# Padding three pools of a three-block transformer kernel so that its tiles begin on multiples of 256 bytes

## The chip, the core and the metric

The kernel runs on one core of a Trainium2 chip, as one launch. The metric is the time of the launch in microseconds on the device. The engines are TensorE (PE in the rows; PEld is its loading of stationary operands), VectorE (DVE), ScalarE (ACT), GpSimd (POOL) and SyncE (SP, which issues most DMAs).

## What is computed

A hybrid mixer layer and two layers of a two-stream transformer, in float32, for 256 tokens of width 1024, plus a second stream of 256 context tokens. Cut to its products, with `rms` the RMS norm:

```
h = x + mixer(rms(x))              # dilated attention, state space scan, gates: w_in, w_attn, w_ssm, w_out
h = h + (silu(n @ w_gate) * (n @ w_up)) @ w_down          # n = rms(h), inner width 2816
x = rms(h)
for layer in (0, 1):
    x, c: half a swiglu                                    # both streams
    x, c: attention (layer 0: windowed and differential; layer 1: latent and neighbourhood)
    x (c in layer 0): half a swiglu
# each part is scaled, shifted and gated by vectors from silu(cond) @ w_mod
```

Nearly all of the arithmetic is products of a weight matrix with 256 tokens.

## The kernel before

**Products.** A weight matrix is cut into slabs: 128 output features with all of their 1024 inputs (or 768, or fewer), 4096 bytes on each of 128 partitions. A slab is loaded into `wraw` (line 102, SyncE), and `split_w` makes two float32r parts of it: `wh` by a cast on ScalarE (line 109) and `wl` by a subtraction on VectorE (line 110). Activations are held feature-major as two such parts too (`ahx` and `alx` for the stream x, `ahc` and `alc` for the context, `hh` and `hl` for the hidden layer of a swiglu, `yn`, `ao` and a few others). `mm3_k` multiplies them: for each block k of 128 inputs three products go to one PSUM tile, `wh·ah` (line 128), `wh·al` (line 129) and `wl·ah` (line 130). In each the 128x128 block of the weight is the stationary operand (512 bytes a partition) and 256 tokens of one block of the activations are the moving one (1024 bytes a partition). Each of the three loads its own stationary operand.

**Order.** `run` takes units (a slab and what is done with it) in order and prepares slabs two units ahead; `wraw`, `wh` and `wl` have five buffers each. With two streams each slab serves 48 products, with one 24. Attention, scan, norm and the vectors of the modulation (line 938, VectorE) are woven in between units. A scheduler sets the order on each engine; it doesn't look at addresses.

**Places.** Tiles are taken from pools, which lie in SBUF one behind the other: `cst` (constants: `ones`, `cols`, `ident`, `tri`, the `mcol` vectors), `raw`, `wsplit`, `tmp`, `small`, then the pools of the streams and of each stage, stacked. Where a tile starts follows from the sizes of all before it. The program's data begins at byte 16,512 of each partition, `cst` is 5,184 bytes long, so `raw` begins at 21,696, which is 84 times 256 and 192 over. In the code that the change touches, `Builder.__init__` (line 68) makes the first pools, `rstd_cols` (line 274) uses `small`, `block1` (line 408) makes `b1x` with `cw` and `half`, and `mix_cd` makes `dqg`.

The end of a branch unit is a place that the prediction uses: `ssm_unit` (line 819) multiplies the 16 blocks of the group norm in one go, 12 of them in the tiles `yn` and the last 4 in `ao_h` and `ao_l`.

Of the kernel before, what the change touches and what calls it, by code (L numbers as in the profile page):

```python
# [8 lines left out]
F32 = mybir.dt.float32  # L9
F32R = mybir.dt.float32r  # L10
AF = mybir.ActivationFunctionType
ALU = mybir.AluOpType
AX = mybir.AxisListType
PSUM = bass.MemoryType.PSUM
# [30 lines left out]
class Unit:  # L45
    """n weight slabs of src from index `at`, and what is done with them for each stream."""
# [5 lines left out]
def weave(units, steps, start=0, stop=0):  # L52
    """The steps spread evenly between the units, from the unit start on, up to stop units before the end."""
    n = len(units) - start - stop
    out, done = list(units[:start]), 0
    for i, u in enumerate(units[start:]):
        out.append(u)
        upto = min(len(steps), -(-len(steps) * (i + 1) // max(n, 1)))
        out += steps[done:upto]
        done = upto  # L60
    return out + list(steps[done:])


class Builder:
# [19 lines left out]

    def pool(self, ctx, name, bufs):
        return ctx.enter_context(self.tc.tile_pool(name=name, bufs=bufs))
# [12 lines left out]
    # ---------------------------------------------------------------- weights  # L99
# [17 lines left out]
    def mm3(self, out, w, acts, m=128, first=True, last=True):  # L117
        """out[m, t] += sum over k of w[k, m] * act[k, t], each factor as the sum of two float32r parts."""
        n = len(acts)
        for k in range(n):  # L120
            self.mm3_k(out, w, acts, k, m, first and k == 0, last and k == n - 1)
# [14 lines left out]
    def stream(self, s, src):  # L136
        """A stream of tokens, feature-major: the residual and what goes into the next product."""
        self.act_p[s] = self.pool(self.ctx, "act" + s, 1)
        self.X[s] = self.act_p[s].tile([128, KB, T], F32, name="x" + s)
        for b in range(KB):  # L140
            self.nc.sync.dma_start(self.X[s][:, b], src[:, b])
# [9 lines left out]
    def lin(self, src, i, acts, evac, m=128, streams=None):  # L151
        """A unit of work: the product of slab i of src with acts(stream), feature-major, to evac(stream, psum)."""
        return Unit(src, i, 1, None, streams, (acts, m, evac))

    def later(self, f, key=None):
        """f is issued behind the next unit of work: TensorE does not wait for what f needs."""
        self.deferred.append((key, f))

    def step(self):
        """What was put off so far."""  # L160
        todo, self.deferred = self.deferred, []
        for _, f in todo:
            f()

    def flush(self, keys=None):
        """What was put off, or only what belongs to the keys, is issued now."""
        while True:
            todo = [d for d in self.deferred if keys is None or d[0] in keys]
            if not todo:
                return  # L170
            self.deferred = [d for d in self.deferred if d not in todo]
            for _, f in todo:
                f()

    def run(self, items, streams, done=None, ko=0, ahead=2):
        """Units in order; the second stream follows the first at a distance, so that the end of one hides
        behind the other. The first ko units go k-outer in the last stream, while its activations are being made.
        Items that are no units are just called."""
# [76 lines left out]
    def background(self, n=1):  # L255
        """The next n pieces of the modulation vectors."""
        for _ in range(min(n, len(self.bg))):
            self.bg.pop(0)()
# [4 lines left out]
    # ------------------------------------------------------------------ norms  # L263
# [10 lines left out]
    def rstd_cols(self, p, n, scale, eps, newton=False):  # L274
        """1 / sqrt(p * scale + eps) of [128, n] sums of squares, a token to a partition."""
# [6 lines left out]
        if newton:  # L282
            # one step on 1 / sqrt(v): r * (1.5 - 0.5 * v * r * r)
# [7 lines left out]
    def sums(self, key):  # L291
        """The sums of squares with a token to a partition."""
# [6 lines left out]
    def on_all(self, r):  # L299
        """A column for each 128 tokens -> the same row on every partition, in PSUM."""  # L300
# [6 lines left out]
    def rstd_all(self, key, width, eps=1e-6):  # L307
        """1 / sqrt(mean of squares + eps) of each token, on every partition (in PSUM)."""
        return self.on_all(self.rstd_cols(self.sums(key), 2, 1.0 / width, eps))

    def norm(self, s, src, scale, shift, h, lo, r):
        """(src * scale) * r + shift of each block, as float32r parts."""
# [10 lines left out]
    def norm_stream(self, s, scale, shift, final=None):  # L323
        """The normed and modulated stream, for the next products; behind the next two units of work.
        final: the gain of a norm of the residual itself that comes first (the sums of its squares: s + "f")."""
# [37 lines left out]
    # -------------------------------------------------------------------- ffn  # L363
    def ffn(self, wg, wu, wds, streams, gate, hid_p, steps, done, after=None):
# [28 lines left out]
        # what a product down needs is ready some units before it  # L393
# [12 lines left out]
# ==================================================================== block 1  # L406
def block1(K, start_mod):
# [8 lines left out]
    # ---- the bias of each head of the dilated attention as a row over the distance, 32 times: read back with  # L416
    # a row pitch shorter by one, it is a Toeplitz tile
# [18 lines left out]
    cw = xpool.tile([128, 120], F32, name="cw")  # L436
# [13 lines left out]
    DIL = (1, 4, 16)  # L450
    o_t = y_t[1:]  # until the convolution needs the place
# [51 lines left out]
    def attend(g, b):  # L503
        """Two heads of a group."""
# [64 lines left out]
    # ---- the weights of the three groups: exp(m_g - max) / sum of den_g * exp(m_g - max)  # L569
    comb = {}  # L570

    def combine_rows():
        # in places that the gates take later
# [114 lines left out]
    # the gates silu(z), twice as large, kept for the four groups  # L688
# [14 lines left out]
    def scan(g):  # L703
        """The state space of a group of 8 heads, in two chunks; then the gate. As steps."""
# [130 lines left out]
    half = xpool.tile([128, 1], F32, name="half")  # L835
    nc.vector.memset(half, 0.5)
# [5 lines left out]
    # ---- the order of it all  # L842
    sctx, qctx, yctx = ExitStack(), ExitStack(), ExitStack()

    def start():
        nc.vector.tensor_scalar(cw, K.cols[:, at:at + 120], 0.5, None, op0=ALU.mult)
# [22 lines left out]
    def mix(a, b):  # L869
        """Two lists of units, evenly."""  # L870
# [52 lines left out]
# ==================================================================== block 2  # L923
def mod_tasks(K, pool, layer, streams):
    """The modulation vectors of one layer, feature-major: mcol[p, i * 8 + b] = (silu(c) @ w_mod + b_mod)[i, b * 128 + p]."""
# [30 lines left out]
class HeadNorm:  # L956
    """RMS norm of a group of heads: feature-major blocks of `rows` partitions with `nh` heads each, their
    gain and rotary embedding. The blocks come one by one; behind the last one the group is finished, a step
    behind each unit of work."""
# [6 lines left out]
    def add(self, p, out):  # L966
        """out: list of (where the heads go, their partitions in p). sums[feature, head]: 1 / width of the head."""
# [31 lines left out]
    def finish(self, i):  # L999
        """The block i, in place."""  # L1000
# [24 lines left out]
def head_selectors(K, pool, width, rows, n):  # L1025
    """sums: 1 / width over the features of a head; sel: the heads of a group onto the features of each block."""
# [10 lines left out]
def stacked(K, pool):  # L1037
    """The two parts of what head norms scale with, one from partition 0, one from 32, nothing elsewhere."""
# [22 lines left out]
def skew(work):  # L1061
    """Items of work in stages: a later stage of an item is issued behind the first one of the next item."""
# [8 lines left out]
def transpose_to(K, pool, blocks, name="pts", bufs=4, eng="v"):  # L1071
    """Up to four [128, 128] blocks, transposed side by side."""
# [13 lines left out]
def v_units(K, src, n, kpb, evac, last):  # L1086
    """Token-major projections: out[token, column], with the activations stationary."""
# [3 lines left out]
    def make(i):  # L1091
        def f(s, slabs):
            for t in range(2):
                if t:
                    K.step()
                # the last unit comes amid the attention
# [21 lines left out]
def mix_ab(K, streams):  # L1118
# [62 lines left out]
    # ---- lambda of the difference  # L1181
# [19 lines left out]
    # ---- A: windowed attention with a sink, four query heads to a key head; two of them at a time  # L1201
# [61 lines left out]
    # ---- B: the difference of two softmaxes, normed by head  # L1263
# [47 lines left out]
    def normed(po):  # L1311
# [4 lines left out]
        # lambda may be huge: the squares are summed 2 ** 64 times smaller, and where the sum itself  # L1316
        # would overflow, the norm is infinite and its inverse zero
# [30 lines left out]
def mix_cd(K, streams):  # L1348
# [8 lines left out]
    free = K.X["c"]  # the residual of the context is not needed any more  # L1357
# [11 lines left out]
    dqg = ap.tile([128, 1], F32, name="dqg")  # L1369
# [15 lines left out]
    # the latent ranks, raw where the values come last  # L1385
# [85 lines left out]
    # the products that are of one stream keep what the other one still reads from being written over  # L1471
# [16 lines left out]
    def attend(b, scores, scale, v, out):  # L1488
        """Two heads of 64, both halves of the queries."""
# [162 lines left out]
# ---- the host: layout only  # L1652
def slabs(w, m=128):
    """[K, M] -> [M / m, 128, (K / 128) * m]: the columns of one block, contiguous on each partition."""
# [5 lines left out]
def vslabs(w, n, kpb):  # L1660
    """[K, N] -> [(N / n) * slabs, 128, kpb * n]; the last slab of a block is padded."""
# [177 lines left out]
```

## Time and profile before

| | |
|---|---|
| time, median of 3 runs | 2555.07 us (2550.63 to 2558.09) |
| profiled execution, first to last instruction | 2558.6 us |
| TensorE busy, products / loads of stationary operands | 2486.2 us (97%) / 2359.6 us (92%) |
| VectorE / ScalarE busy | 1656.2 us (65%) / 1082.6 us (42%) |
| read from HBM | 357.34 MB, a mean of 141 GB/s with the writes |
| mean granted TensorE clock | 0.985 |

The profile gives no time of its execution besides the span; the span lies 3.5 us above the median of the timed runs and 0.5 us above the slowest. Busy times are of the union of an engine's instructions. A product on TensorE is recorded for some 0.28 us although the next starts after some 0.12 us: they are pipelined, so the spacing of starts is the measure, not the length of one.

### The profile page before, as it was taken

What the parts mean: (1) busy time and instruction counts of PE and PEld (TensorE: products, weight loads), DVE (VectorE), ACT (ScalarE), POOL (GpSimd) and SP (SyncE); (2) the same over time, 40 slices, a digit from 0 to 9 for tenths busy, and PEclk for the clock granted to TensorE, in tenths of its full rate; (3) what the DMA queues carried; (4) which work ended last, traced back from release to release, by engine and by line L of the source; (5) the groups of instructions that cost most, each with busy time, mean ns of one, the idle gap of its engine ahead of it and who ended that gap; (6) DMA issues with size and microseconds to landing.
All of it is one profiled execution on the core that took longest, in us unless ns stands there. A gap on an engine that the chain in (4) does not pass through costs nothing.

```text
span 2558.6 us, 48101 instructions
## 1 busy us (share of the span) xinstructions
PE 2486.2 (97%) x19910; PEld 2359.6 (92%) x19910; DVE 1656.2 (65%) x3135; ACT 1082.6 (42%) x2057; POOL 15.7 (1%) x20
## 2 busy tenths in 40 slices
PE   6999999999999999999999999999999987999999
PEld 6999899999999999996599999999999987866999
DVE  4667787787766665768766666566454464667554
ACT  4557565535522322536743222243222243555443
POOL 0000000000000000000000000000000000000000
PEclk9999899999999999999999999999999998999999
DMA  7444455676444443331025444425455433332553
GB/s 225 148 155 160 133 165 188 209 246 202 153 160 159 161 154 120 122 113 59 1 71 167 157 158 158 143 98 165 149 167 163 135 92 80 105 95 81 173 181 124
DMA packets 117242, 364.28 MB, mean 142 GB/s; under 512 B 21050, under 2 KB 28730, under 8 KB 117024
## 3 DMA queue, kind: packets, MB, share of 16 engines
q1 hardware_dynamic: 114512, 355.73, 42.7%
q0 software_dynamic: 1008, 3.09, 1.0%
q8 instruction: 156, 2.56, 0.4%
q10 hardware_dynamic: 1504, 2.40, 0.3%
q14 instruction: 62, 0.51, 0.1%
HBM read 357.34 MB, written 3.82 MB: 141 GB/s over the span
## 4 chain that ended last, share of the span: by engine, by line
PE 59%; DMA 8%; DVE 5%; issue 2%; ACT 1%; DVEq 0%; ACTq 0%; SPq 0%
PE pm L128 17%; PE pm L129 16%; PE pm L130 16%; DMA wraw<-w_mod 7%; DVE junk L938 3%; DVE wl L110 2%; PE pt L1077 1%; DMA sin<-mla_sin 1%; PE pa L984 1%; PE pt L1008 1%; PE pa L1524 1%; PE pm L1276 1%; PE pm L1216 1%; PE pa L1292 0%; PE pm L1532 0%
## 5 line engine op out<-in xcount | busy, mean ns | idle before, releaser
L128 PE MATMUL pm<-ahx,wh 128*128 128x256 f32 x2936 | 841.7, 289 | 17.6 <-ACT q L483 8.0
L109 ACT CAST wh<-wraw 128x1024 fp32r<-128x1024 f32 (+4 forms) x535 | 539.9, 1012 | 707.1 <-PE pm L129 440.0
L129 PE MATMUL pm<-alx,wh 128*128 128x256 f32 x2936 | 834.9, 285 | 0.1
L130 PE MATMUL pm<-ahx,wl 128*128 128x256 f32 x2936 | 834.8, 285 | 0.0
L110 DVE TENSOR_TENSOR wl<-wraw,wh 128x1024 fp32r<-128x1024 f32 (+4 forms) x535 | 627.8, 1176 | 206.7 <-ACT wh L109 205.2
L128 PEld LDWEIGHTS pm<-ahx,wh 128*128 128x128 f32 x2936 | 558.3, 191 | 28.4 <-ACT q L483 8.2
L129 PEld LDWEIGHTS pm<-alx,wh 128*128 128x128 f32 x2936 | 560.5, 191 | 4.5 <-issue 2.7
L130 PEld LDWEIGHTS pm<-ahx,wl 128*128 128x128 f32 x2936 | 559.5, 191 | 2.7 <-issue 2.0
L128 PE MATMUL pm<-ahc,wh 128*128 128x256 f32 x1280 | 361.7, 284 | 4.4 <-ACT ahc L320 4.4
L130 PE MATMUL pm<-ahc,wl 128*128 128x256 f32 x1280 | 360.8, 282 | 0.0
L129 PE MATMUL pm<-alc,wh 128*128 128x256 f32 x1280 | 360.3, 282 | 0.0
L938 DVE SCALAR_TENSOR_TENSOR junk<-wraw,cactc 128x1024 f32<-128x1024 f32 x112 | 137.1, 1224 | 237.9 <-DMA wraw<-w_mod 237.9
L938 DVE SCALAR_TENSOR_TENSOR junk<-wraw,cactx 128x1024 f32<-128x1024 f32 x144 | 175.8, 1221 | 118.6 <-DMA wraw<-w_mod 117.6
L128 PE MATMUL pm<-hhx,wh 128*128 128x256 f32 x880 | 248.9, 283 | 0.0
L130 PE MATMUL pm<-hhx,wl 128*128 128x256 f32 x880 | 248.2, 282 | 0.0
L129 PE MATMUL pm<-hlx,wh 128*128 128x256 f32 x880 | 247.7, 281 | 0.0
L128 PEld LDWEIGHTS pm<-ahc,wh 128*128 128x128 f32 x1280 | 240.7, 189 | 6.8 <-ACT ahc L320 5.0
L130 PEld LDWEIGHTS pm<-ahc,wl 128*128 128x128 f32 x1280 | 241.5, 189 | 0.3
L129 PEld LDWEIGHTS pm<-alc,wh 128*128 128x128 f32 x1280 | 241.2, 189 | 0.6 <-DVE alc L321 0.2
L128 PEld LDWEIGHTS pm<-hhx,wh 128*128 128x128 f32 x880 | 165.9, 188 | 0.2 <-DVE xx L401 0.2
L129 PEld LDWEIGHTS pm<-hlx,wh 128*128 128x128 f32 x880 | 166.0, 189 | 0.0
L130 PEld LDWEIGHTS pm<-hhx,wl 128*128 128x128 f32 x880 | 165.6, 188 | 0.0
(465 smaller groups left out, 3339.2 us busy)
## 6 DMA issues: line engine op xcount, KB each, us to landing
wraw<-w_mod SPq DMA_DIRECT2D x144, 512.0 KB, 4.3
wraw<-f1g SPq DMA_DIRECT2D x44, 512.0 KB, 3.5
wraw<-f1u SPq DMA_DIRECT2D x44, 512.0 KB, 3.5
wraw<-f2g SPq DMA_DIRECT2D x44, 512.0 KB, 3.5
wraw<-f2u SPq DMA_DIRECT2D x44, 512.0 KB, 3.6
wraw<-f1d SPq DMA_DIRECT2D x32, 512.0 KB, 3.9
wraw<-f2d SPq DMA_DIRECT2D x32, 512.0 KB, 3.5
wraw<-w_xbc SPq DMA_DIRECT2D x24, 512.0 KB, 3.5
```

Of the source, the lines that this page charges most:

```text
L109: nc.scalar.copy(h[:, :f], raw[:, :f])
L110: nc.vector.tensor_tensor(lo[:, :f], raw[:, :f], h[:, :f].bitcast(F32), op=ALU.subtract)
L128: nc.tensor.matmul(out, h[:, c], ah, start=first, stop=False)
L129: nc.tensor.matmul(out, h[:, c], al, start=False, stop=False)
L130: nc.tensor.matmul(out, lo[:, c], ah, start=False, stop=last)
L938: nc.vector.scalar_tensor_tensor(junk, raw, 1.0, K.cact[s], op0=ALU.mult, op1=ALU.mult, accum_out=K.mcol[layer, s][:, j:j + 1])
L984: nc.tensor.matmul(self.p[:, c:c + nh], sq[self.rows, j * 128:(j + 1) * 128], self.sums, start=True, stop=True)
L1008: nc.tensor.matmul(r, self.sel[:, cs], self.r, start=True, stop=True)
L1077: nc.tensor.transpose(p[:, j * 128:(j + 1) * 128], b, K.ident)
L1216: nc.tensor.matmul(p[:, :nk], qa[s][rows, 2 * half + b, t * 128:(t + 1) * 128], ka[rows, k0:k0 + nk], start=True, stop=True)
L1276: nc.tensor.matmul(p[:, :nk], qb[s][rows, hd, t * 128:(t + 1) * 128], kb[rows, hd, k0:k0 + nk], start=True, stop=True)
L1524: nc.tensor.matmul(po[64 * e:64 * e + 64, :T], v[:, i, b * 128 + e * 64:b * 128 + e * 64 + 64], pts[i][:, e * 256:e * 256 + 256], start=i ...
```

## The change

Five paddings, of which two are wider tiles in which only the old columns are used; the texts of comments and docstrings are also gone, and lines from 85 on move down by 3 or 4 (line 128 is 131 in the new kernel). The instructions, their order on each engine and their waits are the same in both programs; what differs is where in SBUF tiles start.

```diff
         self.ident = self.cst.tile([128, 128], F32, name="ident")
 
+        self.cst.tile([128, 16], F32, name="pad_cst")
+        self.small.tile([128, 32], F32, name="pad_small", bufs=1)
+
...
-    cw = xpool.tile([128, 120], F32, name="cw")
+    cw = xpool.tile([128, 128], F32, name="cw")
...
     half = xpool.tile([128, 1], F32, name="half")
+    xpool.tile([128, 40], F32, name="pad_x")
     nc.vector.memset(half, 0.5)
...
-        nc.vector.tensor_scalar(cw, K.cols[:, at:at + 120], 0.5, None, op0=ALU.mult)
+        nc.vector.tensor_scalar(cw[:, :120], K.cols[:, at:at + 120], 0.5, None, op0=ALU.mult)
...
-    dqg = ap.tile([128, 1], F32, name="dqg")
+    dqg = ap.tile([128, 64], F32, name="dqg")[:, :1]
```

Where tiles start, as the remainder of the byte address by 256, in the two programs:

| tiles | before | after |
|---|---|---|
| `wraw`, `wh`, `wl`, the tiles of `tmp` (`acc`, `sq`, `g`, `y`) | 192 | 0 |
| `xx`, `ahx`, `alx`, `xc`, `ahc`, `alc`, `hh*`, `hl*` | 64 | 0 |
| `y0` to `y3`, `bt`, `ct`, `aoh`, `aol` (`ao_h`, `ao_l`) | 32 | 0 |
| `ynh*`, `ynl*`, tiles of block 1's attention and scan | 128 | 0 |
| layer 0's attention: `qa*`, `qb*`, `ka`, `kb` | 64 | 0 |
| layer 1's: `qc`, `kc`, `kd`, `vc`, `vd`, `hq*`, `lq*`, `hk*`, `lk*` | 96 | 0 |
| `sel64` and `rh` of layer 0 | 128 | 64 |
| `ident` / `cols` / `cact*`, `junk` | 32 / 128 / 224 | the same |

Blocks inside a tile of weights or activations lie 512 or 1024 bytes apart and share its remainder, except 96-wide slabs (384 bytes apart). Counted over the 17,544 products of lines 128 to 130, the moving operand starts before 64 past a multiple of 128 in 16,872, on a multiple of 128 in the 288 of `yn`, 32 past one in the 192 of `ao`, and 96 past one in 192; the stationary one 64 past a multiple of 128 in all. After, all moving operands start on a multiple of 256, and all stationary ones too but 108 of the 96-wide slabs, which start 128 past one.

## Rows read from the trace of the kernel before

**Rows 1.** Page, part 1: busy us, share of the span, instructions by engine.

```profile
PE 2486.2 (97%) x19910; PEld 2359.6 (92%) x19910; DVE 1656.2 (65%) x3135; ACT 1082.6 (42%) x2057; POOL 15.7 (1%) x20
```

**Rows 2.** Stretches: us, busy us (instructions) by engine, granted clock, DMA share, GB/s.

```profile
512.00:576.00 64.00, 64.00 (x541) 63.99 (x540) 54.51 (x84) 24.02 (x32) 0.00 (x0) 1.00 0.73 245
704.00:832.00 128.00, 128.00 (x1081) 128.00 (x1080) 83.91 (x143) 32.99 (x52) 0.00 (x0) 1.00 0.49 161
1792.00:1920.00 128.00, 128.00 (x1081) 128.00 (x1080) 62.78 (x103) 32.75 (x52) 0.00 (x0) 1.00 0.49 160
```

**Rows 3.** Waits: who waited for whom, us in total, times, longest us.

```profile
PE pt L295 <- DVE acc L272: 22.0, 5, 15.4
...
PE pm L130 <- DVE wl L110: 0.7, 1, 0.7
...
ACT wh L109 <- PE pm L129: 440.0, 223, 5.8
```

**Rows 4.** Groups of TensorE products of line 128: xcount, busy us, mean ns, idle before.

```profile
L128 PE MATMUL pm<-ahx,wh 128*128 128x256 f32 x2936 | 841.7, 289 | 17.6 <-ACT q L483 8.0 <-ACT ahx L320 6.2 <-ACT ahx L114 2.0
...
L128 PE MATMUL pm<-ahc,wh 128*128 128x256 f32 x1280 | 361.7, 284 | 4.4 <-ACT ahc L320 4.4
...
L128 PE MATMUL pm<-hhx,wh 128*128 128x256 f32 x880 | 248.9, 283 | 0.0
...
L128 PE MATMUL pm<-hhc,wh 128*128 128x256 f32 x528 | 148.7, 282 | 0.0
...
L128 PE MATMUL pm<-ynh,wh 128*128 128x256 f32 x96 | 26.7, 279 | 0.0
...
L128 PE MATMUL pm<-aoh,wh 128*128 128x256 f32 x64 | 18.6, 291 | 0.3 <-ACT aoh L114 0.3
```

**Rows 5.** TensorE in order (start us, us): one swiglu unit's 24 products, and the next.

```profile
1799.74 0.28 PE L128 MATMUL pm<-ahc,wh 128*128 128x256 f32 x1
...
1802.59 0.28 PE L128 MATMUL pm<-ahx,wh 128*128 128x256 f32 x1
```

**Rows 6.** TensorE in order: one branch unit, 36 products of `yn`, 12 of `ao`.

```profile
411.73 0.28 PE L128 MATMUL pm<-ynh,wh 128*128 128x256 f32 x1
...
412.08 0.28 PE L128 MATMUL pm<-ynh,wh 128*128 128x256 f32 x1
...
415.83 0.28 PE L128 MATMUL pm<-aoh,wh 128*128 128x256 f32 x1
...
417.25 0.28 PE L128 MATMUL pm<-ynh,wh 128*128 128x256 f32 x1
```

**Rows 7.** TensorE in order: 31 products of `yn` in another branch unit.

```profile
401.34 0.29 PE L130 MATMUL pm<-ynh,wl 128*128 128x256 f32 x1
...
404.99 0.28 PE L128 MATMUL pm<-aoh,wh 128*128 128x256 f32 x1
```

**Rows 8.** TensorE in order: 27 products of a down projection.

```profile
599.78 0.28 PE L128 MATMUL pm<-hhx,wh 128*128 128x256 f32 x1
...
603.02 0.28 PE L128 MATMUL pm<-hhx,wh 128*128 128x256 f32 x1
```

**Rows 9.** TensorE in order: twelve loads for products of two columns, and the next load.

```profile
1073.26 1.43 PEld L984 LDWEIGHTS pa<-cols,sq 128*128 128x128 f32 x12
1073.37 1.39 PE L984 MATMUL pa<-cols,sq 128*128 128x2 f32 x12
...
1074.60 0.19 PEld L128 LDWEIGHTS pm<-ahc,wh 128*128 128x128 f32 x1
```

**Rows 10.** TensorE in order: products of 320 columns, nine apart.

```profile
1139.73 0.31 PE L1102 MATMUL pm<-wh,ahc 128*128 128x320 f32 x1
...
1141.05 0.31 PE L1102 MATMUL pm<-wh,ahc 128*128 128x320 f32 x1
```

## The prediction

> **What bounds the kernel now.** I read the page's busy shares first: TensorE has products in flight for 97% of the span, VectorE works 65% and ScalarE 42% of it [rows 1]. [...] The waits agree: the split weights held TensorE up once, for 0.7 us, while ScalarE, which makes them, waited 440 us for TensorE to give weight buffers back [rows 3]. So the weights, their DMAs and their splitting run ahead, and the length of the kernel is mostly the number of products times the spacing of their starts. The last view is therefore TensorE in order of time, where that spacing is read.
>
> The six groups shown [rows 4] are 5,784 products of line 128; lines 129 and 130 have as many, which makes 17,352 (192 more, in small groups, are left aside).
>
> **The spacing of starts.** In a swiglu unit 24 products start in 1802.59 - 1799.74 = 2.85 us, 118.8 ns each [rows 5]; their moving operands lie 64 bytes past a multiple of 128. [...]
>
> [...] In one branch unit the same two slabs are multiplied with `yn`, which begins on a multiple of 128, and with `ao`, 32 past one. The 12 products of `ao` take 417.25 - 415.83 = 1.42 us, 118.3 ns each. The 36 of `yn` take 415.83 - 411.73 = 4.10 us, 113.9 ns each; without the first three, which still carry the rhythm of the `ao` ahead, 33 in 3.75 us, 113.6 ns [rows 6]. Weights, engines and DMAs beside them are the same, and the unit repeats. [...]
>
> **The change part by part.** *No instruction is added, removed or moved*, so nothing is queued behind anything new, and the two paddings in `cst` and `small` (64 and 128 bytes), like those in `b1x` and at `dqg`, cost only space. What remains is three effects of addresses.
>
> *Moving operands, lines 128 to 130.* 17,352 products less the 288 of `yn`, which are there already, are 17,064; I take 17,000. Each goes from 118.8 to 113.6 ns: 5.2 ns times 17,000 = 88.4 us. All of it is on the path, since the path is this row of products.
>
> *Stationary operands.* They lie 64 past a multiple of 128 before, for `yn` as for all, so no row shows an aligned one under these products. [...] The nearest row is the one with loads alone: the norm of the heads starts twelve loads of 128 columns, each for a product of two, and they are (1074.60 - 1073.26) / 12 = 111.7 ns apart [rows 9]. [...] Those twelve are themselves 64 past a multiple of 128, so the row doesn't settle whether 111.7 is an aligned load's price too. I take no further gain: 111.7 is the nearest row, and nothing in it says that its start has a share in it.
>
> *The rest.* The products of 320 columns are 192: by the same 5.2 ns 1.0 us; another 240 products of 256 columns with the weights as moving operand: 1.2 us. VectorE and ScalarE lose or gain nothing that counts: both are off the path. Where cover thins is the stretch from 512 us, where VectorE works 54.51 of 64 us and the DMA engines move 245 GB/s [rows 2]. With products 4.4% closer VectorE would need 54.51 / 61.2, 89%; it still fits, but queues grow, and I take back the gain of that stretch, 64 x 4.4% = 2.8 us. The waits for norms, the attention and the start keep their length.
>
> **The sum.** 88.4 + 2.2 - 2.8 = 87.8 us. Against the profiled span: 2558.6 - 87.8 = 2470.8. The median of the timed runs is 3.5 us below that span: 2555.1 - 87.8 = 2467.3, so 2467.
>
> **The rivals.**
>
> *The load gets faster too.* [...] For it speaks that every load under these products is misaligned before and none after; against it, that loads with nothing else to slow them still took 111.7 [rows 9]. Chance 0.33, most of it nearer to 2435. [...]
>
> *The rhythm locks at the slower beat.* One of the eight branch units ran `yn` at (404.99 - 401.34) / 31 = 117.7 ns [rows 7], aligned moving operand and all, so the spacing depends also on how loads and products fall against each other. If 117.7 became the rule, 1.1 x 17,000 = 19 us are gained: 2536. If half the units ran so, 2502. Seven of eight units against it. Chance 0.10.
>
> *No change.* If `yn` was faster for something else than its start (it lies high in SBUF), nothing moves: 2555. Against it: in one unit, with the same slabs, it is the operand alone that differs [rows 6]. That the paddings miss their aim is excluded by the addresses of the new program. Chance 0.07. [...]
>
> *Slower: equal remainders collide.* Before, weights and activations differ by 128 in their remainder by 256; after, both start at 0, so the two streams into TensorE ask for like places at like times. Were that to hold them in the slowest steady beat that the trace has, 27 products in 603.02 - 599.78 = 3.24 us, 120.0 ns [rows 8], 1.2 x 17,000 = 20 us would be lost: 2575. It decides from a spacing of 119.3 ns up (0.3% of the time is 7.7 us, 0.45 ns a product). Against it: the streams already run through many remainders within a product, and `yn` with a difference of 64 ran fastest. Chance 0.05.
>
> **How the numbers follow.** My forecast has 0.45, between 2450 and 2490. A change under 0.3%, 7.7 us, is about what a measurement can't tell from none. Faster: 0.45 + 0.33 + 0.10 = 0.88; same 0.07; slower 0.05. The range reaches down to 2390, which takes in most of the faster load, and up to 2512, which takes in half of the locked beat: some 0.8.
>
> **What will tell.** In the stretches of [rows 2] 128 us should hold some 1,127 products (128 / 0.1136) where they are 1,081; above 1,160 the load was the other half. In the branch units `ao` should be as fast as `yn`. The count of waits for split weights shows whether VectorE or the DMAs are the new bound in the stretch from 512 us, or in block 1 as a whole. It is wrong from the ground if the spacing stays at 118.8 ns with all operands on multiples of 256.

## The result, and the profile after

| | before | after |
|---|---|---|
| time, median of 6 runs each, on one chip | 2556.58 us (2549.60 to 2561.60) | 2572.29 us (2569.40 to 2576.80) |
| ratio, with its 95% interval | | 1.0062 (1.0043 to 1.0081) |
| span of the profiled execution | 2558.6 us | 2571.0 us |
| mean granted TensorE clock | 0.985 | 0.985 |

The change makes the kernel slower by 0.6%, some 16 us, where the prediction had 88 us less. The lowest time after lies above the highest before. It came out at the place of the rival that had a chance of 0.05, "equal remainders collide", at 2575.

The page's first part looks as it did [rows 1]: TensorE is as full as before, only 18 us longer.

```profile
PE 2503.8 (97%) x19910; PEld 2378.6 (93%) x19910; DVE 1659.1 (65%) x3135; ACT 1089.1 (42%) x2057; POOL 15.6 (1%) x20
```

The table of stretches (columns as in [rows 2]) tells it at once: at the full granted clock and without idle time, 128 us hold 1,069 products where they held 1,081, and where the prediction wanted 1,127. (The view counts the two products that are in flight when a stretch begins too; spacings below go by starts.)

```profile
512.00:576.00 64.00, 64.00 (x535) 64.00 (x535) 52.12 (x80) 25.52 (x34) 0.00 (x0) 1.00 0.74 247
704.00:832.00 128.00, 128.00 (x1069) 128.00 (x1069) 80.17 (x135) 33.04 (x51) 0.00 (x0) 1.00 0.49 161
1792.00:1920.00 128.00, 128.00 (x1069) 128.00 (x1068) 62.97 (x100) 33.06 (x51) 0.00 (x0) 1.00 0.47 157
```

TensorE in order of time (start us, us) shows the spacing itself. This is a branch unit as in [rows 6]: 36 products of `yn` from 412.34, 12 of `ao` from 416.66.

```profile
412.34 0.28 PE L131 MATMUL pm<-ynh,wh 128*128 128x256 f32 x1
...
416.66 0.28 PE L131 MATMUL pm<-aoh,wh 128*128 128x256 f32 x1
...
418.10 0.28 PE L131 MATMUL pm<-ynh,wh 128*128 128x256 f32 x1
```

4.32 us / 36 and 1.44 us / 12 are both 120.0 ns, where they were 113.6 and 118.3. `ao` did become like `yn`, but `yn` became slow. In the swiglu unit that answers [rows 5], from 1799.44 to 1802.32, 24 products take 2.88 us, 120.0 ns again. It is no longer a mixture: before, single spacings in that unit ran from 115 to 122 ns with a mean of 118.8; after, they are 120 one by one.

Over the whole trace I took all starts that follow a product of the three lines within 140 ns: 17,016 with a mean of 118.77 ns before, 17,048 with 119.90 ns after. 1.13 ns times 17,000 are 19.2 us. Most of the difference to the 12.4 us of the spans is one wait: TensorE's for `q` in block 1 was 8.0 us [rows 4] and is 1.3. In the view of waits (who for whom, us in total, times, longest us) the split weights still run ahead, and ScalarE waits longer for TensorE to give buffers back than in [rows 3], 540.6 us against 440.0: it is still the products that hold the kernel.

```profile
ACT wh L112 <- PE pm L132: 540.6, 269, 5.9
...
PE pm L131 <- ACT q L486: 1.3, 1, 1.3
```

### The profile page after: what moved, and what is told of

Its sections match the earlier page's. It is cut to its first block, busy times and chain, and to the rows that moved or that the text cites. A ratio compares the mean times of both kernels' runs of the same rounds, so it can differ in the third digit from the quotient of the medians.

```text
span 2571.0 us, 48101 instructions
## 1 busy us (share of the span) xinstructions
PE 2503.8 (97%) x19910; PEld 2378.6 (93%) x19910; DVE 1659.1 (65%) x3135; ACT 1089.1 (42%) x2057; POOL 15.6 (1%) x20
## 4 chain that ended last, share of the span: by engine, by line
PE 71%; DMA 1%; ACT 1%; DVE 1%; issue 0%; SPq 0%; ACTq 0%
PE pm L131 21%; PE pm L132 21%; PE pm L133 21%; PE pt L1081 1%; DMA sin<-mla_sin 1%; PE pa L988 1%; PE pm L1280 1%; PE pt L1012 1%; PE pa L1528 1%; PE pm L1220 1%; PE pa L1296 1%; PE pa L1257 0%; PE pm L1536 0%; PE pm L1558 0%; PE pm L1106 0%
## 5 line engine op out<-in xcount | busy, mean ns | idle before, releaser
L112 ACT CAST wh<-wraw 128x1024 fp32r<-128x1024 f32 (+4 forms) x535 | 539.4, 1011 | 800.7 <-PE pm L132 540.6
L131 PEld LDWEIGHTS pm<-ahx,wh 128*128 128x128 f32 x2936 | 566.5, 194 | 22.9 <-ACT ahx L323 7.3
L132 PEld LDWEIGHTS pm<-alx,wh 128*128 128x128 f32 x2936 | 568.6, 194 | 4.3 <-issue 2.4
L133 PEld LDWEIGHTS pm<-ahx,wl 128*128 128x128 f32 x2936 | 568.1, 194 | 2.1 <-issue 1.4
```

The lines of the kernel that those rows point to most:

```text
L112: nc.scalar.copy(h[:, :f], raw[:, :f])
L131: nc.tensor.matmul(out, h[:, c], ah, start=first, stop=False)
L132: nc.tensor.matmul(out, h[:, c], al, start=False, stop=False)
L133: nc.tensor.matmul(out, lo[:, c], ah, start=False, stop=last)
```

## The experiments

Throughout, *distance* is the remainder by 256 of where the moving operand starts less where the stationary one starts. Before, all weights lay on 192, so `ahx` and its like (on 64) had distance 128, `yn` (on 128) 192, and `ao` (on 32) 96; after, all have distance 0. Three theories stood against each other. **D**: the distance decides the spacing (in the first two expectations with a period of 128 or of 256). **S**: stationary operands on a multiple of 256 are slow, and aligned moving ones would be fast without that. **M**: the moving operand's own start decides, with 0 slow and 128 fast.

**Four placements.** Each is the changed kernel with only the two pads in `cst` and `small` different. The runs of before on that chip had a median of 2560.17 us (21 runs).

Weights on 0, activations on 64:

```diff
-        self.small.tile([128, 32], F32, name="pad_small", bufs=1)
+        self.small.tile([128, 48], F32, name="pad_small", bufs=1)
```

> The new kernel with 64 bytes more padding behind the weights: weights at remainder 0 by 256, all activations at 64. Numbers are the spacing of the products of 256 columns (120.0 ns in the new kernel, 118.8 before, 113.6 for yn before) and the time. Theory D (the difference of the two addresses decides: 64 apart by 128 is fast, 0 is slow): 113.3 to 113.6 ns, 6.5 x 17,352 = 113 us less than the new kernel, about 2459 us. Theory S (a stationary operand on a multiple of 256 is what is slow): 120 ns, 2572 us. Theory M (the moving operand's own address decides, and only 128 past a multiple of 256 is fast): 118.8 ns as before, about 2556 us. If the difference counts by 256 and not by 128 (yn began 192 past its weights, here it is 64), this one may stay slow while weights 64 past the activations are fast.

Measured: 2550.93 us (2544.33 to 2556.46), ratio 0.9965 (0.9948 to 0.9982); mean spacing 117.56 ns.

Weights on 0, activations on 128 (distance 128, as most had before, but both aligned to 128 bytes):

```diff
-        self.small.tile([128, 32], F32, name="pad_small", bufs=1)
```

> The change without its padding of the pool small: weights at remainder 0, all activations at 128, so every operand still starts on a multiple of 128. Theory D with a period of 128: difference 0 as in the new kernel, 120.0 ns, 2572 us; with a period of 256 the difference is 128, as it was for ahx before: 118.8 ns, 2556 us. Theory S: 120 ns, 2572 us. Theory M: 113.4 ns, since the moving operand is where yn was, about 2457 us. My own prediction's step (a moving operand on a multiple of 128 is fast) also asks for 113.6 ns here.

Measured: 2558.33 us (2550.41 to 2562.52), ratio 0.9996 (0.9979 to 1.0014); mean spacing 118.77 ns, as before, with the same mixture of 115 to 122.

Weights and activations on 192 (distance 0, nothing aligned):

```diff
-        self.cst.tile([128, 16], F32, name="pad_cst")
```

> The change without its padding of the pool cst: weights and activations both at remainder 192, so neither is on a multiple of 128, and their difference is 0 as in the new kernel. Theory D: 120.0 ns, 2572 us. Theory S (only an aligned stationary operand is slow): back to 118.8 ns, 2556 us. Theory M: 118.8 ns, 2556 us.

Measured: 2575.79 us (2571.73 to 2582.34), ratio 1.0062 (1.0032 to 1.0093); mean spacing 119.91 ns.

Weights on 64, activations on 0 (distance 192):

```diff
-        self.cst.tile([128, 16], F32, name="pad_cst")
-        self.small.tile([128, 32], F32, name="pad_small", bufs=1)
+        self.cst.tile([128, 32], F32, name="pad_cst")
+        self.small.tile([128, 80], F32, name="pad_small", bufs=1)
```

> All activations at remainder 0 by 256 as in the new kernel, weights at 64: the difference is that of yn before (192 by 256). Theory D: 113.3 to 113.6 ns, about 2459 us, whether the period is 128 or 256. Theory S: about 113.5 ns too, since the load is off the multiple and the moving operand on it. Theory M: 120.0 ns, 2572 us.

Measured: 2538.71 us (2532.62 to 2542.04), ratio 0.9918 (0.9885 to 0.9951); mean spacing 115.25 ns.

The stretch from 1792 us of the four, in that order:

```profile
1792.00:1920.00 128.00, 128.00 (x1088) 127.89 (x1087) 63.06 (x103) 32.91 (x52) 0.00 (x0) 1.00 0.51 161
```

```profile
1792.00:1920.00 128.00, 128.00 (x1081) 128.00 (x1080) 61.92 (x102) 33.41 (x52) 0.00 (x0) 1.00 0.49 161
```

```profile
1792.00:1920.00 128.00, 128.00 (x1069) 128.00 (x1068) 62.07 (x104) 32.69 (x52) 0.00 (x0) 1.00 0.49 156
```

```profile
1792.00:1920.00 128.00, 126.49 (x1103) 125.89 (x1102) 63.40 (x104) 31.75 (x52) 0.00 (x0) 1.00 0.51 162
```

S falls with the third: no operand is on a multiple of 256, and the beat is the slow one of the changed kernel (1,069, 120.0 ns). M falls with the second: the moving operands start on 128, as `yn` did, and nothing gets faster (1,081). D with a period of 128 falls with the first two: it asked for 113.5 ns and then for 120.0. D with a period of 256 is what is left. It asked for 118.8 and 120.0 in the second and third, and these came. In the fourth it had the direction but not the size: 115.25 ns and 2538.71 us, where it asked for some 113.5 and 2459. There 113.3 ns did come, but for little more than half of the products, and waits took part of what they gave (both below). In its branch unit, weights on 64 and activations on 0, `yn` and `ao` run alike, and fast: 4.08 us / 36 and 1.36 us / 12 are 113.3 ns.

```profile
412.20 0.28 PE L131 MATMUL pm<-ynh,wh 128*128 128x256 f32 x1
...
416.28 0.28 PE L131 MATMUL pm<-aoh,wh 128*128 128x256 f32 x1
...
417.64 0.28 PE L131 MATMUL pm<-ynh,wh 128*128 128x256 f32 x1
```

**Two scans within one kernel.** If it is the distance, operands at different places must run at different speeds side by side, with the same weights. In the first scan `stream` and the two swiglu pools each get a pad:

```diff
         self.act_p[s] = self.pool(self.ctx, "act" + s, 1)
+        self.act_p[s].tile([128, 40 if s == "x" else 16], F32, name="pad_act" + s)
...
         hid_p = K.pool(fctx, "h1", 14)
+        hid_p.tile([128, 16], F32, name="pad_h1", bufs=1)
...
         hid_p = K.pool(fctx, "h2", 14)
+        hid_p.tile([128, 32], F32, name="pad_h2", bufs=1)
```

> The changed kernel (weights on 0, remainder by 256) with small paddings, so that the moving operands of different stages lie at different remainders: x 160, c 224, hidden layer of the first swiglus 32, of the second 96; before these, spacings known by distance (moving less stationary, modulo 256): 0 120.0 ns, 64 117.6, 128 118.8, 192 113.3 to 117.7. Theory D (the distance alone decides, with period 256): within one kernel the spacing of starts changes from operand to operand, 32 and 160 near 117.7 (from layer 1 of the kernel before, where distances 32 and 160 stand), 96 near 118.3 to 119.4 (from ao, distance 96), and 224 somewhere between 113.3 and 120, since it lies between 192 and 0. Rival R (the weights' own place decides together with the whole layout): with weights on 0 all four stay between 118.8 and 120, as in the three kernels so far that have... only remainder 0 or 192 for them.

The second has its pads at 40 (x only), 56 and 48, and takes both parts of an activation from one tile, from 16 bytes on:

```diff
-        h = self.act_p[s].tile([128, n, T], F32R, name="ah" + s, tag="ah")
-        lo = self.act_p[s].tile([128, n, T], F32R, name="al" + s, tag="al")
-        return h, lo
+        a = self.act_p[s].tile([128, 2 * n * T + 8], F32R, name="ah" + s, tag="ah")
+        a = a[:, 4:4 + 2 * n * T].rearrange("p (h n t) -> p h n t", h=2, t=T)
+        return a[:, 0], a[:, 1]
```

> As the scan before, with weights on 0: x at 176, c at 208 (both parts of an activation in one tile that is used from 16 bytes on), hidden layer of the first swiglus at 192, of the second at 160. Theory D: the hidden products of the first swiglus at 113.3 to 117.7 ns, as at the same distance of 192 with the weights on 64; the second's near the 117.7 of distance 160; x and c between. If the effect goes in steps of 64 bytes, 208 behaves like 192 and 176 like 128 (118.8); if it is smooth, both lie near 113.3 to 117.7. Rival R (192 was fast because the weights lay on 64): 118.8 or more for the hidden products too.

Single runs: 2562.92 and 2557.45 us, mean spacings 118.17 and 118.06 ns. Products of the first scan, TensorE in order: in the second swiglu of layer 0, 24 of the context at distance 224 (from 1472.65) and 24 of the hidden layer at 96 (from 1475.49); in the first of layer 1, 24 of the hidden layer at 32 (from 2056.36).

```profile
1472.65 0.28 PE L131 MATMUL pm<-ahc,wh 128*128 128x256 f32 x1
...
1475.49 0.28 PE L131 MATMUL pm<-hhx,wh 128*128 128x256 f32 x1
...
1478.37 0.28 PE L131 MATMUL pm<-ahc,wh 128*128 128x256 f32 x1
...
2056.36 0.28 PE L131 MATMUL pm<-hhx,wh 128*128 128x256 f32 x1
...
2059.16 0.28 PE L131 MATMUL pm<-hhc,wh 128*128 128x256 f32 x1
```

2.84, 2.88 and 2.80 us: 118.3, 120.0 and 116.7 ns. In the second scan, 24 products of the hidden layer at 192, with the weights on 0:

```profile
770.15 0.28 PE L131 MATMUL pm<-hhx,wh 128*128 128x256 f32 x1
...
772.87 0.28 PE L131 MATMUL pm<-hhc,wh 128*128 128x256 f32 x1
```

2.72 us, 113.3 ns. Rival R, for which weights on 0 stay above 118.8, falls here; both kernels change their beat from one operand to the next. Where I had expected figures I missed three: 32 is 116.7 and not 117.7; 96 is no 118.3 but 120.0 in a long row, as slow as distance 0; and 176 and 208 are neither like 128 nor like 192, so the effect does not go in steps of 64 bytes. All distances seen, with the steady spacings of long rows of products:

| distance | ns between starts | seen in |
|---|---|---|
| 0 | 120.0 | after; weights and activations on 192 |
| 32 | 116.7 | first scan, hidden layer |
| 64 | 117.8, in seven short stretches 113.3 | activations on 64 |
| 96 | 120.0 | first scan, hidden layer (12 in a row before: 118.3) |
| 128 | 118.5 to 118.8, in some stretches 120.0 | before; activations on 128 |
| 160 | 117.3 to 118.8, in one stretch 120.0 | both scans (hidden layer, x) |
| 176 | 119.2 | second scan, x |
| 192 | 113.3 or 117.8 | `yn` before; weights on 64; second scan |
| 208 | 118.1 (mean; 117.3 to 119.1) | second scan, context |
| 224 | 118.3 | first scan, context and block 1's hidden layer |

So a distance does not fix one spacing: some distances have two or three, and something else picks among them. The kernel with weights on 0 and activations on 128, distance 128 throughout, holds 1,069 products in one stretch and 1,081 in another; and before, the last swiglu ran as slowly as after the change (last row).

```profile
480.00:608.00 128.00, 128.00 (x1069) 128.00 (x1068) 105.98 (x160) 56.03 (x79) 0.00 (x0) 1.00 0.75 251
2400.00:2528.00 128.00, 128.00 (x1081) 128.00 (x1080) 73.42 (x91) 55.92 (x77) 0.00 (x0) 1.00 0.58 181
```

```profile
2400.00:2528.00 128.00, 128.00 (x1069) 128.00 (x1069) 73.12 (x90) 55.46 (x76) 0.00 (x0) 1.00 0.55 180
```

Even the same program does not repeat it. The fourth kernel, run again on another chip (below), took 4.24 us / 36 = 117.8 ns for the `yn` of a branch unit of the kind that took 113.3 ns above:

```profile
411.88 0.28 PE L131 MATMUL pm<-ynh,wh 128*128 128x256 f32 x1
...
416.12 0.28 PE L131 MATMUL pm<-aoh,wh 128*128 128x256 f32 x1
```

What the distance decides is which spacings occur and how often: at 0 only 120.0 in long rows of 128x128 blocks; at 192, in the first profiled execution of the fourth kernel, single spacings of up to 114 ns for 57% of the products. What picks the beat is open.

**Where most of the fourth kernel's gain went.** 3.52 ns times 17,000 are 60 us of spacing, yet its span fell by 23 us. Waits of TensorE grew, above all for VectorE's `g`, which empties a PSUM tile (line 380, before line 377; 1.1 us there), and for `xc`, `wl` and `xx`; the one for `e` is as before:

```profile
PE pm L131 <- DVE g L380: 7.6, 15, 1.3
...
PE pm L131 <- DVE xc L404: 4.3, 5, 1.4
PE pm L1280 <- ACT e L1061: 3.2, 4, 1.5
PE pm L133 <- DVE wl L113: 3.0, 4, 0.8
PE pm L131 <- DVE xx L404: 2.9, 4, 1.1
```

And VectorE in order shows why it comes late to `g`: it stands 3.16 us for the modulation's slab (line 942, before line 938) and does `g` only behind that.

```profile
857.25 1.23 DVE L113 TENSOR_TENSOR wl<-wraw,wh 128x1024 fp32r<-128x1024 f32 x1
861.64 1.23 DVE L942 SCALAR_TENSOR_TENSOR junk<-wraw,cactc 128x1024 f32<-128x1024 f32 x1 [3.16 <-DMA wraw<-w_mod]
862.79 0.08 DVE L942 DVE_READ_ACCUMULATOR junk<-wraw,cactc 128x1 f32 x1
862.79 0.41 DVE L380 TENSOR_TENSOR g<-g,pm 128x256 f32<-128x256 f32 x1
```

TensorE starts again when that `g` is done:

```profile
863.26 0.38 PE L131 MATMUL pm<-ahc,wh 128*128 128x256 f32 x1 [0.47 <-DVE g L380]
```

Theory V says that this standing takes the gain back; rival N that norms, attention and clock do. The test lets VectorE multiply a tile that is always there, so that the modulation is not computed; the slabs are still loaded. It was made in the kernel before and in the fourth kernel:

```diff
-                nc.vector.scalar_tensor_tensor(junk, raw, 1.0, K.cact[s], op0=ALU.mult, op1=ALU.mult,
+                nc.vector.scalar_tensor_tensor(junk, K.cact["c"], 1.0, K.cact[s], op0=ALU.mult, op1=ALU.mult,
```

> The kernel before, in which VectorE forms the modulation vectors from a tile that is always there (the vector of the context) in place of the slab just loaded: its instructions are as many and as long, the slabs are still loaded, but VectorE does not stand still for them. What is computed of the modulation is left out that way. Theory V (in the kernel with faster products VectorE, standing for a modulation slab, delays what frees PSUM tiles, and that eats the gain): here TensorE was never held by it, so the time stays within 6 us of before, 2550 to 2560. Rival N (the gain is lost at norms, attention and the clock): the same.

Measured: 2566.41 us (2554.14 to 2572.58, 8 runs; before 2561.76), ratio 1.0013 (0.9990 to 1.0035): above the 2550 to 2560 that I had written, but not different from before.

> The same change in the kernel with weights on 64 and activations on 0, whose products were 3.5 ns closer, 60 us in the sum, while its span fell by 23 us. The modulation vectors are formed from a tile that is always there, with the slabs still loaded. Theory V: the waits of TensorE for g, xc and xx go, and 15 to 35 us with them: 2500 to 2523. Rival N: the time stays at 2533 to 2542.

Measured: 2507.02 us (2503.84 and 2510.21), ratio 0.9778 (0.9718 to 0.9837). Between these two kernels the spacing falls from 118.63 to 115.24 ns; 3.39 times 17,000 are 58 us. The time falls by 59 us between the medians, of 8 runs and of 2, and by 46 us between the two profiled executions from which the spacings are (spans of 2554.6 and 2508.1 us). This speaks for V: without VectorE's standing, most of a gain in spacing arrives, perhaps all. With the old spacing the standing costs nothing that shows. Of TensorE's waits for `g`, `xc` and `xx`, 14.8 us in the fourth kernel, 1.5 are left there. The test took away more than the waiting, though: with nothing to wait for, the scheduler put 231 of the 256 multiplications of the modulation between 500 and 1,000 us, where the fourth kernel has 103. How much of the effect is the standing and how much the other order was not separated.

**Two attempts to have that in a whole kernel.** Both keep weights on 64, activations on 0, and compute everything. The first has each piece of the modulation load the slab of the next piece before it works on its own (`more` says that another piece follows in the same row):

```diff
-            raw = K.load_raw(K.A[f"w_mod{layer}"][j])
+            raw = K.next_raw or K.load_raw(K.A[f"w_mod{layer}"][j])
+            K.next_raw = None
+            if more and j < 71:
+                K.next_raw = K.load_raw(K.A[f"w_mod{layer}"][j + 1])
```

> Weights on 64 and activations on 0 (distance 192) as in the fourth kernel, and the slab of the modulation vectors is asked for one piece earlier: a piece loads the slab of the next piece before VectorE works on its own, wherever the next piece is in the same row of pieces. Everything is computed. Theory V (VectorE's standing for these slabs is what holds TensorE back there): most of the 31 us that came when nobody waited for them comes here too, 2508 to 2525 us, and the waits of TensorE for g, xc and xx shrink. Rival B (the slab held longer takes one of five buffers from the weights, so that TensorE waits for split weights instead): 2533 or more, with waits for wl.

> The fourth kernel once more, on the same chip as the one with the earlier loads, for a comparison: 2533 to 2543 us, as before.

Measured: 2536.96 us (2526.07 to 2541.33), ratio 0.9883 (0.9856 to 0.9910), against 2537.98 us (2523.70 to 2552.76), ratio 0.9877 (0.9843 to 0.9912), for the fourth kernel beside it. It changes nothing. The time is that of rival B, but B's sign is missing: TensorE waits 1.9 us for `wl`, where it was 3.0 in the fourth kernel. VectorE still stands for the slabs:

```profile
DVE junk L947 <- DMA wraw<-w_mod: 345.3, 123, 4.7
```

In the fourth kernel that row reads 363.3 us, 131 times. Most of these loads stand earlier in SyncE's order, but by one to three places only, and the scheduler had moved most of VectorE's instructions for them forward too, so this run did not test the buffer. The second attempt gives the slabs two buffers of their own during the swiglus:

```diff
-    def load_raw(self, src):
-        t = self.raw_p.tile([128, 1024], F32, name="wraw")
+    def load_raw(self, src, mod=False):
+        t = (self.mod_p if mod and self.mod_p else self.raw_p).tile([128, 1024], F32, name="wraw")
...
         hid_p = K.pool(fctx, "h1", 14)
+        K.mod_p = K.pool(fctx, "mrawh1", 2)
```

> Weights on 64 and activations on 0 (distance 192) as in the fourth kernel; during the swiglus the slabs of the modulation vectors have two buffers of their own, so that such a load waits only for the slab two before it and not for the rotation of the five that the weights use. Everything is computed. Theory V with the buffer as the cause of the late slab: VectorE's standing for these slabs (363 us there) falls by more than half, TensorE's waits for g, xc and xx go, 2508 to 2525 us. Rival O (VectorE's order is set so that it comes to a slab as soon as a plan thinks it there, whatever buffer it has): VectorE stands as long as before, and the time is 2533 or more.

Measured: 2530.92 us (2520.19 to 2543.51), ratio 0.9887 (0.9859 to 0.9915; before 2561.32). The mechanism did what it should: VectorE's standing fell to 50.0 us,

```profile
DVE junk L945 <- DMA wraw<-w_mod: 50.0, 50, 4.1
```

and the two-stream swiglus hold 1,131 and 1,132 products in 128 us, 113.3 ns, a little more than the 1,127 that the prediction had wanted of the change:

```profile
704.00:832.00 128.00, 128.00 (x1131) 128.00 (x1131) 78.79 (x127) 34.46 (x55) 0.00 (x0) 1.00 0.46 146
...
1792.00:1920.00 128.00, 128.00 (x1132) 128.00 (x1131) 48.42 (x71) 34.93 (x54) 0.00 (x0) 1.00 0.32 99
```

Part of that is the beat and not the buffers: from 704 us the fourth kernel had no idle time either, but its slow beat, 117.8 ns. And the whole is hardly better than the fourth kernel; the stretches of 500 us show two places. The fourth kernel, then this one:

```profile
0.00:500.00 500.00, 473.53 (x3896) 447.01 (x3897) 355.90 (x635) 290.81 (x571) 3.77 (x10) 0.96 0.55 174
...
1000.00:1500.00 500.00, 489.62 (x3711) 435.52 (x3710) 344.41 (x797) 223.98 (x481) 0.00 (x0) 0.99 0.33 102
```

```profile
0.00:500.00 500.00, 464.65 (x3810) 438.22 (x3811) 361.19 (x649) 285.92 (x564) 3.77 (x10) 0.95 0.56 179
...
1000.00:1500.00 500.00, 482.19 (x3603) 425.98 (x3602) 400.06 (x909) 219.30 (x473) 0.00 (x0) 0.98 0.41 130
```

From 1000 us, around layer 0's attention, VectorE works 400 us instead of 344, and TensorE starts 108 products fewer: with the new buffers the scheduler put more of the modulation there. And the clock stood at its lower level, 0.5 of the full, for longer: summed over the records, 128 us in this execution, 94 in the fourth kernel's, 77 in that of before and in the one without the standing (the last at 2508.1 us of span). At that level the products of the three lines start 213.0 ns apart in the kernel before (the median of each lower record that holds any; one row of them starts at 469.42, 469.63 and 469.84 us), where they have 113.3 here at the full clock; if TensorE had work throughout, 51 us more of it cost up to 51 x (1 - 113.3 / 213.0) = 24 us, an estimate. One such place can be read. At the end of block 1's mixer TensorE waits 7.60 us for the sums of squares of a norm, where it waited 2.75 in the fourth kernel:

```profile
466.48 0.98 PE L300 MATMUL pt<-ones,acc 128*128 128x1 f32 x4 [7.60 <-DVE acc L277]
```

VectorE is busy for 19.46 of the 20 us from 460 us and has multiplications of the modulation among these sums in its order; from 461.6 us the clock stands at its lower level for 17.1 us (a mean of 0.57 over these 20 us), where the fourth kernel had 6.8. So there work that was moved forward delays a norm. Which weighs more, the new place of the modulation or the clock, was not tried.

## Why the prediction was wrong, point by point

**What bounds the kernel: right.** The time is mostly the number of products times the spacing of their starts. The runs bear it out, and the two kernels without the standing most plainly: 58 us of spacing, 46 to 59 us of time.

**The spacing depends on addresses: right.** 113.3 to 120.0 ns for the same product, with the same instructions, on nothing but padding.

**The step that failed is the one on the moving operands**: all of them are taken to the 113.6 ns of `yn`, as if a product were fast wherever its moving operand starts on a multiple of 128. It was read from `yn` against `ao` in one unit [rows 6]. But in the kernel before all stationary operands of these products but 108 lay on the same remainder, 192. So over that trace the start of the moving operand and its distance to the stationary one are the same quantity but for a constant, and no row shown could tell them apart. I read the comparison as one of starts; it was one of distances: 192 for `yn`, 96 for `ao`. The 118.3 ns of `ao`, 32 past a multiple, are those of 12 products; over the whole trace `ao` has some 119.4 ns. The change moved both operands, set the distance to 0 for all, and with it the term of 88.4 us turned into a loss of 19. The activations on 128 with the weights on 0 settle it: there the start that made `yn` fast brings nothing, 118.77 ns.

**The stationary operands: right to take no gain for their own start.** The spacing followed the distance: 119.90 and 119.91 ns at 0, with the weights on 0 and on 192, and 118.77 at 128, with the weights on 192 and on 0. The loads by themselves [rows 9] are as slow when their tiles are on multiples of 256: from 1072.61 to 1073.96 twelve of them take 1.35 us, 112.5 ns, where they took 111.7 (the rows are given to 0.01 us, which is 0.8 ns here).

```profile
1072.61 1.43 PEld L988 LDWEIGHTS pa<-cols,sq 128*128 128x128 f32 x12
1073.96 0.19 PEld L131 LDWEIGHTS pm<-ahc,wh 128*128 128x128 f32 x1
```

Two figures of the prediction reach below 113.6 ns: the lower end of the range, 2390, some 109 ns a product, and the count of 1,160, 110.3 ns. No run shows long rows of these products at such a spacing: the fastest long stretch, in the kernel with buffers for the modulation, held 1,132 products in 128 us, 113.3 ns, and that kernel took 2530.92 us. The 2435 of the faster load asks for the 111.7 ns of the loads alone [rows 9]; no stretch of products came to that either.

**The rival "equal remainders collide" had the right quantity and the price**: slowest steady beat 120.0 ns, 2575 us; measured 120.0 ns and 2572.29. That the two streams collide is not shown: the price was that of a beat already in the trace, and 96 apart is as slow as 0. Its chance of 0.05 was the second mistake. I set two sentences against it. That the streams run through many remainders within a product is no argument: no row shows how the two move against each other on the way. And that `yn` "with a difference of 64 ran fastest" should have spoken for it: it says that the spacing goes by the difference. I also gave the difference without its sign; 64 ahead ran at 117.8 ns almost throughout, 64 behind (distance 192) at 113.3 for more than half of the products.

**The beat that locks: right as a warning.** Distance 192 has both beats, 113.3 and 117.8, as [rows 6] and [rows 7] had; in the fourth kernel the stretch from 704 us has the slow one, that from 2448 us the fast one. And distance 128 has 120.0 beside 118.7: [rows 8] and [rows 5] already showed both at the same remainders, a sign that neither start nor distance is the whole. The prediction's reason, how loads and products fall against each other, was a guess that no row shows; what chooses between the beats is open.

**The conversion of spacing into time.** The prediction took back 2.8 us where cover thins. For the fourth kernel it was some 37 of 60 us, and not only in the stretch that I had named for VectorE's load: elsewhere VectorE has time to spare (63.40 of 128 us busy from 1792 us), but it stands in order for a transfer, 363.3 us in all, while PSUM tiles wait behind it (`g` behind the 3.16 us above). A busy share of a half [rows 2] says nothing of that. In the trace TensorE's waits for `g`, `xc` and `xx` are 14.8 of the 37 us, 1.3 before; the clock's longer time at the lower level, 94 us against 77, is up to 17 x (1 - 115.25 / 213.0) = 8, an estimate; the rest was not taken apart.

## What to carry to other kernels

Where an operand's place seems to matter, ask for the place relative to what: the two operands of a product have a distance, and aligning both to the same boundary gave the slowest spacing here, 120.0 ns. A comparison inside a trace separates two causes only if the trace varies them apart; where it does not, give both readings a real chance, above all when the change moves both. And before a gain on the bounding engine is counted in full, look for an engine beside it that stands in order for a transfer with that engine's buffers queued behind it: here VectorE stood 363.3 us for slabs, and of 60 us of spacing 23 arrived.

## What was not expected of the hardware

For products of 256 float32r columns, each with a new 128x128 stationary operand, the spacing went with the distance of the two operands' start addresses in these runs: 120.0 ns at 0 and 96, 116.7 at 32, mostly 118.7 but also 120.0 at 128, mostly 117.8 but also 113.3 at 64, and 113.3 or 117.8 at 192, by stretch and by execution. It isn't smooth: 176 and 208, 16 bytes on either side of 192, have 119.2 and 118.1. Two distances 256 apart ran alike: the 192 of the fourth kernel and of the second scan are 192 and 448 modulo 512, and both have 113.3 (4.08 us / 36 and 2.72 us / 24). Why 192 has the fastest beat, and what picks the beat, no run here tells. The best kernels made from this that compute everything, with weights on 64 and activations on 0, are 0.8 to 1.2% faster than before (ratios 0.9918 and 0.9877 and, with buffers of its own for the modulation, 0.9887).
